# The opening of a two-layer decoder kernel: layer 0's first modulation sums go from VectorE to TensorE, and their tiles' places, the loads and the opening blocks are put in another order

## The chip, the cores and the metric

The kernel runs on one core of one Trainium2 chip. The metric is the device time of one execution in microseconds (us). Engines are named as in the profile: PE (TensorE's products), PEld (its weight loads), DVE (VectorE), ACT (ScalarE), POOL (GpSimd), SP (SyncE, which issues most DMAs).

## The reference, cut to what matters

A decoder trunk of two layers on x of 1024 tokens by 1024 channels, in f32. Every layer begins with an RMS norm, scaled and shifted by numbers that come from a vector c:

```
cond = silu(c)
mod = cond @ ada_w[i] + ada_b[i]              # 1024 -> 3 x 1024
shift, scale, gate = split(mod, 3)
h = rmsnorm(x, norm_g[i]) * (1 + scale) + shift
p = h @ w_in                                  # layer 0: 29 column tiles of 128
...                                           # RWKV-7 heads and chunked gMLP (layer 0), attention (layer 1)
x = x + gate * (y @ w_out)
```

The change concerns the shift and scale of layer 0: a product of the 1024 numbers of cond with a 1024 x 2048 part of ada_w[0]. Nothing of h exists before the first of these sums are there.

## The kernel before, in words

All large products take operands that are split into two float32r parts, hi and lo (hi is the rounded value, lo the rest), and three products (hi x hi, lo x hi, hi x lo) stand for one in f32. Tokens are worked in two halves of 512 (HT). h is kept transposed: 8 row blocks k of 128 channels, each 128 x 512 for a half, in the tiles hi0, lo0, hi1, lo1 of the pool hp (new_hh).

The opening stage stands in the pool st0. The order of PE's instructions is as the code writes it (manual_schedule); on DVE, ACT, POOL and SP a scheduler orders by its own estimate, and the DMAs that are marked keep_in_program_order stay as written. Every engine takes its queue in order.

- xnorm(b) loads 128 tokens of x and scales them by their RMS (squares on ACT, a power on POOL, the scaling at L338 on ACT for b of 4 and above, at L340 on DVE below). xblock(b) transposes blocks 0 to 3 on PE (xtp) and copies them to xT on ACT (L352).
- wpiece(i, g) loads half of one of the four first weight tiles (wr) and splits it: hi on ACT (L358), lo on POOL (L359).
- ada_first(q), q of 0 to 3, makes the sums for two row blocks k = 2q and 2q + 1: four loads of 128 x 1024 (adaraw, four buffers, so that a load waits until DVE has read an earlier one), eight steps on DVE acc = raw * cond + acc (L373 the first, L371 the other seven), and four products adac of acc with a column of ones, which add up the 128 partitions. Three small DVE instructions (L382 to L384) make the columns bcol and scol.
- hbuild(k) makes h of the first half: a scale and shift on DVE (hf, L393), hi on ACT (L388), lo on POOL or DVE (L389).
- first(k) is the opening group: for each of four accumulators (p0, p1, pM, py) three products with row block k, 12 products of 512 columns. It runs for k = 0 to 7.
- hlate(k) makes h of the second half from x blocks 4 to 7: four transposes into one of two PSUM buffers (tag m), hf on ACT (L402) or DVE (L404), then hi and lo as in hbuild.

Behind first(7) the four accumulators are read: lora_evac and krv_evac (shifted, ACT L302, DVE L303; tanh of lora at L315). Then front(0) begins: two products lw and la of lora with wupt, each into a buffer of tag m, th and tha on ACT (L509, L513) that empty them, and a transpose kt. Only behind kt stands the first product of the second half (pproj, gproj), with which the long stream of products starts that lasts to the end of the kernel.

Of the kernel before, what the change touches and what calls it, by code (L numbers as in the profile page):

```python
# [93 lines left out]
def tile_kernel(ctx, tc, x, cons, par, rows, ada, ada0, ew, wup, sgw, sgb, ewo, ow, owo, out, dbg=None):  # L94
# [43 lines left out]
    def pm(name):  # L138
        return ps.tile([P, HT], F32, name=name, tag="m", bufs=2)
# [143 lines left out]
    def new_h():  # L283
        return [new_hh(half) for half in range(2)]

    h = new_h()
# [42 lines left out]
    ws = [[wp.tile([P, KC, P], F32R, name="w" + n, tag="w" + n, bufs=2) for n in ("hi", "lo")] for i in range(2)]  # L329
    ws += [[u1.tile([P, KC, P], F32R, name="w", tag=t, bufs=1) for t in ts] for ts in (("SV", "AR"), ("PA", "BR"))]  # L330
    with tc.tile_pool(name="st0", bufs=1, side="right", reuse_waits="tile") as sp, tc.manual_schedule(engines={nc.tensor.engine}):
        def xnorm(b):
            xt = sp.tile([P, D], F32, name="x0", tag="x", bufs=4)
            d = nc.sync.dma_start(out=xt, in_=x[b * P:(b + 1) * P, :])
            tc.keep_in_program_order(d)
            rs = rms_scale((xt[:, 0:HT], xt[:, HT:D]), sp, pg)
            if b >= 4:
                S.activation(xt, xt, AF.Copy, scale=rs)  # L338
            else:
                V.tensor_scalar(out=xt, in0=xt, scalar1=rs, scalar2=None, op0=ALU.mult)  # L340
            return xt

        xT = sp.tile([P, KC, HT], F32, name="xT")
# [1 line left out]
        def xblock(b):  # L345
            xt = xnorm(b)
            for g in range(2):
                pt = pm("xtp")
                for i in range(4):
                    k = g * 4 + i  # L350
                    transpose(pt[:, i * P:(i + 1) * P], xt[:, k * P:(k + 1) * P], ident)
                S.activation(xT[:, g * 4:g * 4 + 4, b * P:b * P + P], pt.rearrange("p (k t) -> p k t", t=P), AF.Copy)  # L352

        def wpiece(i, g):
            gs = slice(g * 4, g * 4 + 4)
            raw = rt.tile([P, 4, P], F32, name="wr", tag="krv", bufs=6)
            tc.keep_in_program_order(nc.sync.dma_start(out=raw, in_=ew[FIRST[i][0]][:, gs, :]))
            S.activation(ws[i][0][:, gs, :], raw, AF.Copy)  # L358
            G.tensor_tensor(out=ws[i][1][:, gs, :], in0=raw, in1=ws[i][0][:, gs, :].bitcast(F32), op=ALU.subtract)  # L359

        def ada_first(q):
            acc = sp.tile([P, 4, P], F32, name="acc", tag="acc", bufs=2)
            for g in range(4):
                raw = sp.tile([P, 2, 4, P], F32, name="adaraw", tag="adaraw", bufs=4)
                d = nc.sync.dma_start(out=raw, in_=ada0[q][:, g])
                tc.keep_in_program_order(d)
                start_dma[0] = d.ins
                for i in range(2):
                    c = cond[:, 2 * g + i:2 * g + i + 1]
                    if g + i:  # L370
                        V.scalar_tensor_tensor(out=acc, in0=raw[:, i], scalar=c, in1=acc, op0=ALU.mult, op1=ALU.add)  # L371
                    else:
                        V.tensor_scalar(out=acc, in0=raw[:, i], scalar1=c, scalar2=None, op0=ALU.mult)  # L373
            pt = psc("adac")
            for i in range(4):
                mm(pt[:, i:i + 1], lhsT=acc[:, i, :], rhs=ones[:, 0:1], start=True, stop=True)
            ks2 = slice(2 * q, 2 * q + 2)

            def col(name):
                return prm[:, COLS[name] + 2 * q:COLS[name] + 2 * q + 2]  # L380

            V.tensor_tensor(out=bcol[:, ks2], in0=pt[:, 0:2], in1=col("sh0"), op=ALU.add)  # L382
            V.tensor_tensor(out=scol[:, ks2], in0=pt[:, 2:4], in1=col("sc0"), op=ALU.add)
            V.scalar_tensor_tensor(out=scol[:, ks2], in0=scol[:, ks2], scalar=1.0, in1=col("ng0"), op0=ALU.add, op1=ALU.mult)  # L384
# [21 lines left out]

        pts = [pproj("p0"), pproj("p1"), pM(), ps.tile([P, HT], F32, name="py", tag="y", bufs=1)]

        def first(k):
            for i in range(4):  # L410
                whi, wlo = ws[i]
                mm(pts[i], lhsT=whi[:, k, :], rhs=h[0][0][:, k, :], start=(k == 0), stop=False)
                mm(pts[i], lhsT=whi[:, k, :], rhs=h[0][1][:, k, :], start=False, stop=False)
# [2 lines left out]
        for b in range(4):  # L416
            xblock(b)
        xs = []
        ada_first(0)
        hbuild(0, G)  # L420
        hbuild(1, G)
        for i in range(4):
            wpiece(i, 0)
        first(0)
        ada_first(1)
        hbuild(2, G)
        hbuild(3, G)
        for i in range(4):
            wpiece(i, 1)
        xs.append(xnorm(4))  # L430
        xs.append(xnorm(5))
        first(1)
        first(2)
        ada_first(2)
        hbuild(4, G)
        hbuild(5, G)
        xs.append(xnorm(6))
        xs.append(xnorm(7))
        first(3)
# [12 lines left out]
        first(7)  # L452
        hlate(6, True, G)
        hlate(7, False, V)
        for i in range(4):
# [956 lines left out]
```

## Time and profile before

| what | value |
|---|---|
| runs, median (lowest to highest of 3) | 1116.17 us (1114.96 to 1116.32) |
| the profiled execution's own time | 1111.06 us |
| its span | 1109.2 us |
| PE busy, of the span | 1028.4 us, 93% |
| DVE / ACT / POOL busy | 720.3 / 526.6 / 388.7 us |
| mean granted clock of PE | 0.988 |

A row of a timeline gives start, length, engine, line, operation, output<-inputs, shapes and count; in brackets stands how long the engine was idle before it, and what ended that. A row of the waits gives who waited for whom, the sum in us, how often, and the longest. Rows of equal instructions that follow each other are merged, so that the length of a merged row reaches from the first start to the last end.

### The profile page before, as it was taken

How to read it: one execution, taken by the hardware profiler on the slowest of the kernel's cores; microseconds unless marked ns; L12 is line 12 of the kernel's file. 1: busy time of each engine (PE TensorE's matmuls, PEld its weight loads, DVE VectorE, ACT ScalarE, POOL GpSimd, SP SyncE). 2: the span in 40 equal slices, each digit the busy share in tenths (PEclk: the TensorE clock that was granted, in tenths of full speed). 3: DMA queues.
4: the chain of work that ended last, by engine and by line, in shares of the span. 5: the costliest groups of instructions: out<-in, count | busy, mean ns of one | idle time of the engine just before them, and what ended most of it. 6: DMA issues, size and time to landing. Idle time of an engine off the chain costs nothing. (4 is left out here: it accounts for less than half of the span.)

```text
span 1109.2 us, 20591 instructions
## 1 busy us (share of the span) xinstructions
PE 1028.4 (93%) x7800; PEld 838.4 (76%) x7800; DVE 720.3 (65%) x1682; ACT 526.6 (47%) x1252; POOL 388.7 (35%) x490
## 2 busy tenths in 40 slices
PE   3799898899998998988999899999999999999997
PEld 2577676777776776766878688878888888878886
DVE  5975858585869584694744576764565654488754
ACT  4575434554454535444332322335565644487521
POOL 3642414240335122252333200034554544467201
PEclk9899999999999999999999999999999999999999
DMA  8710212122222121123324543321110111252121
GB/s 311 267 27 20 77 59 67 40 66 61 75 79 66 59 87 49 58 69 107 102 80 141 161 143 124 124 72 40 39 39 20 39 38 39 69 171 74 62 93 57
DMA packets 55130, 93.41 MB, mean 84 GB/s; under 512 B 5748, under 2 KB 15988, under 8 KB 55032
## 3 DMA queue, kind: packets, MB, share of 16 engines
q1 hardware_dynamic: 45032, 77.10, 21.5%
q10 hardware_dynamic: 10000, 15.01, 4.2%
q8 instruction: 61, 1.00, 0.4%
q14 instruction: 37, 0.30, 0.1%
HBM read 79.49 MB, written 12.59 MB: 83 GB/s over the span
## 5 line engine op out<-in xcount | busy, mean ns | idle before, releaser
L118 PE MATMUL pproj<-hi,whi 128*128 128x512 f32 x704 | 284.5, 404 | 0.7 <-ACT vt L1177 0.7
L118 PE MATMUL pproj<-lo,whi 128*128 128x512 f32 x704 | 283.6, 403 | 0.0
L118 PE MATMUL pproj<-hi,wlo 128*128 128x512 f32 x704 | 283.5, 403 | 0.0
L246 POOL TENSOR_TENSOR wlo<-wraw,whi 128x512 fp32r<-128x512 f32 x86 | 115.1, 1358 | 181.1 <-ACT whi L245 180.2
L118 PEld LDWEIGHTS pproj<-hi,whi 128*128 128x128 f32 x704 | 133.5, 190 | 26.6 <-issue 1.7
L118 PEld LDWEIGHTS pproj<-hi,wlo 128*128 128x128 f32 x704 | 133.3, 189 | 25.1 <-issue 1.0
L118 PEld LDWEIGHTS pproj<-lo,whi 128*128 128x128 f32 x704 | 133.3, 189 | 24.3 <-issue 0.9
L245 ACT ACTIVATE whi<-wraw 128x512 fp32r<-128x512 f32 x102 | 58.6, 622 | 65.7 <-PE htp L122 31.3
L118 PE MATMUL op<-wo,whi 128*128 128x512 f32 x256 | 80.8, 397 | 0.0
L1213 ACT ACTIVATE Sx<-Sx,nm 128x257 f32<-128x257 f32 (+1 forms) x128 | 62.3, 489 | 27.2 <-DVE nm L1209 25.5
L1209 DVE CUSTOM_DVE_ANT_0 Sx<-pS,bias,nsink 128x256 f32<-128x256 f32 (+1 forms) x128 | 53.4, 463 | 30.1 <-PE pS L118 28.6
L1217 POOL TENSOR_SCALAR Sx<-Sx,rc 128x256 f32<-128x256 f32 (+1 forms) x128 | 60.0, 485 | 25.7 <-DVE rc L1215 23.2
L1229 DVE TENSOR_TENSOR PL<-pT,PH 128x512 fp32r<-128x512 f32 (+1 forms) x64 | 41.6, 654 | 30.0 <-ACT PH L1228 29.5
L118 PEld LDWEIGHTS op<-wo,whi 128*128 128x128 f32 x256 | 48.4, 190 | 11.2 <-issue 0.3
L857 DVE SCALAR_TENSOR_TENSOR adacc<-araw,cond,adacc 128x512 f32<-128x512 f32 x56 | 47.0, 839 | 12.6 <-DMA araw<-ada 12.5
L118 PE MATMUL op<-hi,yl 128*128 128x512 f32 (+1 forms) x136 | 51.8, 381 | 0.4 <-DVE yl L1328 0.4
L118 PE MATMUL op<-hi,yh 128*128 128x512 f32 (+1 forms) x136 | 51.8, 381 | 0.4 <-ACT yh L1327 0.4
L118 PE MATMUL op<-lo,yh 128*128 128x512 f32 (+1 forms) x136 | 51.5, 379 | 0.0
L118 PE MATMUL op<-wo,wlo 128*128 128x512 f32 x128 | 51.2, 400 | 0.0
L213 POOL TENSOR_TENSOR st<-st,nhalf 128x1 f32<-128x1 f32 x16 | 10.4, 650 | 102.6 <-DVE st L212 102.6
L650 DVE TENSOR_TENSOR pr<-Lf,LT 128x2 f32<-128x2 f32 (+14 forms) x120 | 44.2, 368 | 2.6
L1228 ACT ACTIVATE PH<-pT 128x512 fp32r<-128x512 f32 (+1 forms) x64 | 35.7, 563 | 17.5 <-PE pT L1223 16.2
(311 smaller groups left out, 2171.7 us busy)
## 6 DMA issues: line engine op xcount, KB each, us to landing
araw<-ada SPq DMA_DIRECT2D x64, 256.0 KB, 2.8
wraw<-ew SPq DMA_DIRECT2D x50, 256.0 KB, 3.1
wraw<-ow SPq DMA_DIRECT2D x36, 256.0 KB, 3.0
adaraw<-ada SPq DMA_DIRECT2D x16, 512.0 KB, 5.5
x<-x SPq DMA_DIRECT2D x8, 512.0 KB, 7.4
woraw<-ewo SPq DMA_DIRECT2D x16, 256.0 KB, 3.0
xr<-x ACTq DMA_DIRECT2D x16, 256.0 KB, 3.2
wraw<-y0d SPq DMA_DIRECT2D x16, 256.0 KB, 3.2
```

The lines of the kernel that those rows point to most:

```text
L118: last[0] = nc.tensor.matmul(out, lhsT=lhsT, rhs=rhs, **kw).ins
L213: G.tensor_tensor(out=st[:, 3:4], in0=st[:, 2:3], in1=nhalf[:, 0:1], op=ALU.pow)
L245: a = S.activation(hi[:, gs, :], raws[g], AF.Copy)
L246: b = E.tensor_tensor(out=lo[:, gs, :], in0=raws[g], in1=hi[:, gs, :].bitcast(F32), op=ALU.subtract)
L650: V.tensor_tensor(out=pr[:, 0:nc_, 0:i + 1], in0=Lf[:, i:i + 1, 0:i + 1].to_broadcast([P, nc_, i + 1]), in1=LTt[:, 0:nc_, 0:i + 1], op=ALU ...
L857: op = V.scalar_tensor_tensor(out=acc, in0=raw, scalar=cond[:, k:k + 1], in1=acc, op0=ALU.mult, op1=ALU.add)
L1209: V.tensor_tensor_reduce(out=Sx[:, e, off:2 * P], in0=pS3[:, e, 0:nk], in1=bias[e][:, off:], scale=1.0, scalar=nsink[:, hd:hd + 1], op0=AL ...
L1213: S.activation(pr[:, e, off:2 * P + 1], Sx[:, e, off:2 * P + 1], AF.Exp, bias=nm[:, e:e + 1], scale=-1.0, accum_out=sm[:, e:e + 1])
L1217: G.tensor_scalar(out=pr[:, e, off:2 * P], in0=pr[:, e, off:2 * P], scalar1=rc[:, e:e + 1], scalar2=0.5, op0=ALU.mult, op1=ALU.mult)
L1228: S.activation(PH[:, ks, :], pT2[:, ks, :], AF.Copy)
L1229: V.tensor_tensor(out=PL[:, ks, :], in0=pT2[:, ks, :], in1=PH[:, ks, :].bitcast(F32), op=ALU.subtract)
```

## The change

The sums become products. For each of the eight steps a product takes as its stationary operand a 128 x 32 tile of c32, of which the first column is cond's and the others are zero, and as its moving operand the loaded 128 x 512 tile itself. Product j goes to the column group j mod 4, that is to 32 of the 128 partitions of one PSUM tile (adar); two products add up in each group. ACT copies the tile to acc, and the four adac products with the ones add the partitions as before (adac is unchanged). The four loads of one q go to one tile; for q of 1 and 2 that is the place of hi1 and lo1, which hold h of the second half later, so new_hh(1) now stands behind the sixth block.

The loads, the opening blocks and some copies are put in another order or on another engine: the x loads 4 to 7 come behind all of ada0; adac of q = 1, 2, 3 stands in the middle of a block (first(k, mid)); all hlate come behind the seventh block, four before the last block and four after; x blocks 4 to 7 are scaled on DVE; half of the xT copies and half of the wlo pieces go to DVE.

```
-            if b >= 4:
-                S.activation(xt, xt, AF.Copy, scale=rs)
-            else:
-                V.tensor_scalar(out=xt, in0=xt, scalar1=rs, scalar2=None, op0=ALU.mult)
+            V.tensor_scalar(out=xt, in0=xt, scalar1=rs, scalar2=None, op0=ALU.mult)
...
+                if g:
+                    V.tensor_copy(dst, src)
+                else:
+                    S.activation(dst, src, AF.Copy)
...
-            G.tensor_tensor(out=ws[i][1][:, gs, :], in0=raw, in1=ws[i][0][:, gs, :].bitcast(F32), op=ALU.subtract)
+            (V if i % 2 else G).tensor_tensor(out=ws[i][1][:, gs, :], in0=raw, in1=ws[i][0][:, gs, :].bitcast(F32), op=ALU.subtract)
...
-                    if g + i:
-                        V.scalar_tensor_tensor(out=acc, in0=raw[:, i], scalar=c, in1=acc, op0=ALU.mult, op1=ALU.add)
-                    else:
-                        V.tensor_scalar(out=acc, in0=raw[:, i], scalar1=c, scalar2=None, op0=ALU.mult)
+        def ada_load(q):
+            if q in (1, 2):
+                raws = hp.tile([P, 4, 2, 4, P], F32, name="adaraw", tag=("hi1", "lo1")[q - 1])
+            else:
+                raws = sp.tile([P, 4, 2, 4, P], F32, name="adaraw", tag="adaraw", bufs=1)
+            for g in range(4):
+                tc.keep_in_program_order(nc.sync.dma_start(out=raws[:, g], in_=ada0[q][:, g]))
+            adas[q] = raws
+
+        def ada_rows(q):
+            raws = adas[q]
+            pt = pm("adar")
+            for g in range(4):
                 for i in range(2):
+                    j = 2 * g + i
+                    a = j % 4 * 32
+                    mm(pt[a:a + 32, :], lhsT=c32[:, j, :], rhs=raws[:, g, i].rearrange("p a b -> p (a b)"), start=j < 4, stop=j >= 4, tile_position=(0, a))
+            acc = rt.tile([P, 4, P], F32, name="acc", tag="t", bufs=5)
+            S.activation(acc, pt.rearrange("p (a b) -> p a b", a=4), AF.Copy)
+            adas[q] = acc
+
+        def ada_done(q):
+            acc = adas.pop(q)
             pt = psc("adac")
...
-        def first(k):
+        def first(k, mid=None):
             for i in range(4):
+                if i == 2 and mid is not None:
+                    ada_done(mid)
...
-        ada_first(0)
-        hbuild(0, G)
-        hbuild(1, G)
+        ada_load(0)
+        ada_rows(0)
+        ada_done(0)
         for i in range(4):
             wpiece(i, 0)
+        ada_load(1)
+        hbuild(0, V)
+        hbuild(1, G)
         first(0)
-        ada_first(1)
-        hbuild(2, G)
+        ada_load(2)
+        ada_rows(1)
+        first(1, 1)
+        hbuild(2, V)
         hbuild(3, G)
         for i in range(4):
             wpiece(i, 1)
-        xs.append(xnorm(4))
-        xs.append(xnorm(5))
-        first(1)
+        ada_load(3)
         first(2)
-        ada_first(2)
-        hbuild(4, G)
+        ada_rows(2)
+        first(3, 2)
+        for b in range(4, 8):
+            xs.append(xnorm(b))
+        hbuild(4, V)
         hbuild(5, G)
-        xs.append(xnorm(6))
-        xs.append(xnorm(7))
-        first(3)
         first(4)
+        ada_rows(3)
+        first(5, 3)
+        hbuild(6, V)
+        hbuild(7, G)
+        h.append(new_hh(1))
+        first(6)
         hlate(0, True, G)
         hlate(1, True, V)
-        ada_first(3)
-        hbuild(6, V)
-        hbuild(7, G)
         hlate(2, False, G)
         hlate(3, True, V)
-        first(5)
+        first(7)
         hlate(4, True, G)
-        hlate(5, False, G)
-        first(6)
-        first(7)
+        hlate(5, False, V)
         hlate(6, True, G)
         hlate(7, False, V)
```

PE's queue at the second block (k = 1), before: the four adac stand ahead of it, and the sums were made on DVE.

```order
L118 MATMUL adac<-ones,acc 128x1 x4
L118 MATMUL p_132<-hi,whi 128x512
L118 MATMUL p_132<-lo,whi 128x512
L118 MATMUL p_132<-hi,wlo 128x512
L118 MATMUL p_133<-hi,whi 128x512
L118 MATMUL p_133<-lo,whi 128x512
L118 MATMUL p_133<-hi,wlo 128x512
L118 MATMUL pM<-hi,w 128x512
```

The same place now; p_133 and p_134 are here what p_132 and p_133 were, the accumulators p0 and p1.

```order
L118 MATMUL adar<-adaraw,c_129 32x512 x8
L118 MATMUL p_133<-hi,whi 128x512
L118 MATMUL p_133<-lo,whi 128x512
L118 MATMUL p_133<-hi,wlo 128x512
L118 MATMUL p_134<-hi,whi 128x512
L118 MATMUL p_134<-lo,whi 128x512
L118 MATMUL p_134<-hi,wlo 128x512
L118 MATMUL adac<-ones,acc 128x1 x4
L118 MATMUL pM<-hi,w 128x512
```

The sums stand ahead of the block, and adac has moved into its middle, with six products ahead of it and six behind. The blocks k = 3 and k = 5 look the same.

ACT's queue from the reading of the first accumulator (lora) on, before; behind these rows come the DMAs of tri and sgwt and then th<-lw, which empties the buffer that kt waits for.

```order
L302 ACTIVATE lora<-p_132,der 128x512
L302 ACTIVATE krv<-p_133,der 128x512
L302 ACTIVATE krv<-pM,der 128x512
L305 ACTIVATE carry<-p_132,prm 128x1
L315 ACTIVATE lora<-lora 64x512
L302 ACTIVATE krv<-py,der 128x512
L505 ACTIVATE kkn<-krv,prm 128x512
L305 ACTIVATE carry<-p_133,prm 128x1
L402 ACTIVATE hf<-xtp,bcol,scol 128x512
L468 DMA rcon<-cons 128x260
L388 ACTIVATE hi<-hf 128x512
L305 ACTIVATE carry<-pM,prm 128x1
```

The same place now, the first twelve rows (L420 is what L402 was, L406 what L388 was, L529 what L505 was).

```order
L302 ACTIVATE lora<-p_133,der 128x512
L420 ACTIVATE hf<-xtp,bcol,scol 128x512
L302 ACTIVATE krv<-p_134,der 128x512
L302 ACTIVATE krv<-pM,der 128x512
L406 ACTIVATE hi<-hf 128x512 x2
L302 ACTIVATE krv<-py,der 128x512
L305 ACTIVATE carry<-p_133,prm 128x1
L315 ACTIVATE lora<-lora 64x512
L529 ACTIVATE kkn<-krv,prm 128x512
L305 ACTIVATE carry<-p_134,prm 128x1
L305 ACTIVATE carry<-pM,prm 128x1
L420 ACTIVATE hf<-xtp,bcol,scol 128x512
```

And the rows that follow, up to the last ahead of th<-lw (which is L533 now).

```order
L305 ACTIVATE carry<-py,prm 128x1
L406 ACTIVATE hi<-hf 128x512 x2
L492 DMA rcon<-cons 128x260
L420 ACTIVATE hf<-xtp,bcol,scol 128x512
L815 DMA tri<-cons 128x128
L822 DMA sgwt<-sgw 128x256
L406 ACTIVATE hi<-hf 128x512
L824 DMA lnb<-rows 128x128
L664 ACTIVATE LT<-rcon 128x128
L406 ACTIVATE hi<-hf 128x512
L827 DMA bst<-sgb 64x128 x2
```

Between lora and th stand three hf and six hi now, where one hf and one hi stood. From the start of the second half's products on, every engine's order is as it was.

More of the change, by code (lines that the diff above doesn't have):

```diff
@@ L284, in new_h @@
         return [new_hh(half) for half in range(2)]
-    h = new_h()
+    h = [new_hh(0)]
     rfs = ExitStack()
@@ L331, in tile_kernel @@
     with tc.tile_pool(name="st0", bufs=1, side="right", reuse_waits="tile") as sp, tc.manual_schedule(engines={nc.tensor.engine}):
+        c32 = sp.tile([P, 8, 32], F32, name="c32")
+        G.memset(c32, 0.0)
+        V.tensor_copy(c32[:, :, 0:1], cond.unsqueeze(2))
         def xnorm(b):
@@ L335, in xnorm @@
             tc.keep_in_program_order(d)
+            start_dma[0] = d.ins
             rs = rms_scale((xt[:, 0:HT], xt[:, HT:D]), sp, pg)
-            if b >= 4:
-                S.activation(xt, xt, AF.Copy, scale=rs)
-            else:
-                V.tensor_scalar(out=xt, in0=xt, scalar1=rs, scalar2=None, op0=ALU.mult)
+            V.tensor_scalar(out=xt, in0=xt, scalar1=rs, scalar2=None, op0=ALU.mult)
             return xt
@@ L351, in xblock @@
                     transpose(pt[:, i * P:(i + 1) * P], xt[:, k * P:(k + 1) * P], ident)
-                S.activation(xT[:, g * 4:g * 4 + 4, b * P:b * P + P], pt.rearrange("p (k t) -> p k t", t=P), AF.Copy)
+                dst, src = xT[:, g * 4:g * 4 + 4, b * P:b * P + P], pt.rearrange("p (k t) -> p k t", t=P)
+                if g:
+                    V.tensor_copy(dst, src)
+                else:
+                    S.activation(dst, src, AF.Copy)
         def wpiece(i, g):
@@ L358, in wpiece @@
             S.activation(ws[i][0][:, gs, :], raw, AF.Copy)
-            G.tensor_tensor(out=ws[i][1][:, gs, :], in0=raw, in1=ws[i][0][:, gs, :].bitcast(F32), op=ALU.subtract)
-        def ada_first(q):
-            acc = sp.tile([P, 4, P], F32, name="acc", tag="acc", bufs=2)
-            for g in range(4):
[L364 to L367, printed above, removed]
-                for i in range(2):
-                    c = cond[:, 2 * g + i:2 * g + i + 1]
-                    if g + i:
-                        V.scalar_tensor_tensor(out=acc, in0=raw[:, i], scalar=c, in1=acc, op0=ALU.mult, op1=ALU.add)
-                    else:
-                        V.tensor_scalar(out=acc, in0=raw[:, i], scalar1=c, scalar2=None, op0=ALU.mult)
+            (V if i % 2 else G).tensor_tensor(out=ws[i][1][:, gs, :], in0=raw, in1=ws[i][0][:, gs, :].bitcast(F32), op=ALU.subtract)
+        adas = {}
+        def ada_load(q):
[3 more added lines that the diff above has]
+                raws = sp.tile([P, 4, 2, 4, P], F32, name="adaraw", tag="adaraw", bufs=1)
+            for g in range(4):
+                tc.keep_in_program_order(nc.sync.dma_start(out=raws[:, g], in_=ada0[q][:, g]))
[4 more added lines that the diff above has]
+            for g in range(4):
+                for i in range(2):
+                    j = 2 * g + i
[6 more added lines that the diff above has]
+            acc = adas.pop(q)
             pt = psc("adac")
```

## The prediction

> **What bounds the kernel now.** I read the windows first, cut at three places of the timeline: the first product of the opening group (28.01), the first product of that group's last row block (66.32) and the first product of the second half (73.61). The columns are length, then busy time of PE, PEld, DVE, ACT, POOL, then the granted clock and the DMA share.
>
> ```profile
> core 0: us, PE busy (x) PEld busy (x) DVE busy (x) ACT busy (x) POOL busy (x), PEclk, DMA share, GB/s
> 0.00:28.01 28.01, 9.74 (x40) 7.82 (x40) 16.68 (x39) 14.11 (x33) 10.39 (x17) 1.00 0.87 310
> 28.01:66.32 38.31, 31.45 (x133) 24.44 (x133) 34.01 (x49) 21.62 (x40) 23.05 (x17) 0.91 0.58 198
> 66.32:73.61 7.29, 6.15 (x30) 4.00 (x28) 4.22 (x6) 7.29 (x16) 4.10 (x5) 1.00 0.17 48
> 73.61:1109.20 1035.59, 981.03 (x7603) 802.10 (x7601) 665.44 (x1589) 483.55 (x1167) 351.14 (x451) 0.99 0.23 74
> ```
>
> From 73.61 on, PE is busy 981.03 of 1035.59 us. The change leaves PE's order there as it was, so I take a shift of 73.61 to be passed on to the end one to one. Everything is decided ahead of 73.61. In the second window DVE is the fullest engine (34.01 of 38.31), and in the third ACT is busy all the time (7.29 of 7.29). Who waits there is in the list of waits up to 74 us, PE's and then the DMA queue's, and what DVE does is in its groups for the same stretch (mean ns behind the busy time):
>
> ```profile
> PE adac L118 <- DVE acc L371: 4.4, 3, 2.8
> PE adac L118 <- DVE st L211: 3.5, 1, 3.5
> PE lw L118 <- ACT krv L302: 1.0, 1, 1.0
> SPq L365 <- DVE acc L371: 19.9, 9, 4.3
> L371 DVE SCALAR_TENSOR_TENSOR acc<-adaraw,cond,acc 128x512 f32<-128x512 f32 x28 | 29.3, 1047 | 0.7
> ```
>
> DVE's 28 accumulations (29.3 us) are what PE waits for, 4.4 + 3.5 = 7.9 us (the small st of L211 stands right behind them), and the queue holds tiles back 19.9 us for them. That is what the change takes away. It could give back those 7.9 us and the slow clock behind them, if nothing else came last.
>
> **The change, term by term.** I follow PE's queue.
>
> *Term 1, up to the first product.*
>
> ```profile
> 17.41 1.94 PE L122 MATMUL xtp<-con,x 128*128 128x128 f32 x8 [1.29 <-DVE x L340]
> 18.53 0.60 ACT L352 ACTIVATE xT<-xtp 128x512 f32<-128x512 f32 x1 [1.78 <-PE xtp L122]
> 22.11 1.84 PE L118 MATMUL adac<-ones,acc 128*128 128x1 f32 x8 [2.76 <-DVE acc L371]
> 35.31 1.02 PE L118 MATMUL adac<-ones,acc 128*128 128x1 f32 x8 [0.65 <-DVE acc L371]
> L118 PE MATMUL adag<-adacc,ones x8: 589/591/592, 430.6 to 624.5; 128*1 128x512 f32 x8
> 430.59 1.02 PE L118 MATMUL adag<-adacc,ones 128*1 128x512 f32 x2
> 152.91 1.15 PE L118 MATMUL pn<-SV,BR 128*64 128x64 f32 x32 [0.62 <-DVE AR L735]
> ```
>
> The new sums (adar, 8 products of 128x32 by 512 in f32) do not occur before. The nearest row is adag, one such product alone: two records, 1.02 us less the 0.59 of the last gives 0.43 from start to start, so 0.86 a product. Eight in a row cost 6.9 us; four side by side, 1.7. That column groups do run side by side shows in pn: 64 of 512 elements would be 0.054 a record, 1.7 us for 32, and they took 1.15 with the last one's drain in it, so two at a time. Nothing shows four; I take 1.7 because pn loses nothing to sharing, and keep 6.9 as the far end. At the start all this doubles, since the clock is half: the same eight adac records take 1.84 there and 1.02 later. So: last transposes end at 17.41 + 1.94 = 19.4; adar 3.4 and a drain of 0.2 make 23.0; ACT's copy 0.6 (as xT), adac 1.8, together 25.5 with the handovers; then the way from adac to the first product, 2.3 (the next fence has it at 2.6 with DVE held up). First product at 27.8, against 28.01. The DVE chain that goes is replaced by a PE-ACT-PE chain as long: gain 0.2.
>
> [...]
>
> *Term 2, up to the last row block.*
>
> ```profile
> 36.37 0.16 DVE L382 TENSOR_TENSOR bcol<-adac,prm 128x2 f32<-128x2 f32 x1
> 37.66 1.00 DVE L393 TENSOR_SCALAR hf<-xT,scol,bcol 128x512 f32<-128x512 f32 x2
> 38.25 0.64 ACT L388 ACTIVATE hi<-hf 128x512 fp32r<-128x512 f32 x1 [2.77 <-DVE hf L393]
> 38.96 1.31 POOL L389 TENSOR_TENSOR lo<-hf,hi 128x512 fp32r<-128x512 f32 x1 [0.71 <-ACT hi L388]
> 40.32 0.50 PE L118 MATMUL p<-lo,whi 128*128 128x512 f32 x1 [0.86 <-POOL lo L389]
> 46.61 1.84 PE L118 MATMUL adac<-ones,acc 128*128 128x1 f32 x8 [3.50 <-DVE st L211]
> 48.88 0.63 PE L118 MATMUL p<-lo,whi 128*128 128x512 f32 x1
> 49.31 0.63 PE L118 MATMUL p<-hi,wlo 128*128 128x512 f32 x1
> 66.32 0.39 PE L118 MATMUL p<-hi,whi 128*128 128x512 f32 x1
> 66.54 0.39 PE L118 MATMUL p<-lo,whi 128*128 128x512 f32 x1
> 69.04 1.03 PE L122 MATMUL xtp<-con,x 128*128 128x128 f32 x8
> ```
>
> A product of 512 starts every 0.23 us, at half clock every 0.43 (48.88 to 49.31, behind a gap of 3.5). PE's own work in the new order, from 27.8: the first block at half clock 12 x 0.43 = 5.2; second sums 2.5 (between 1.7 and 3.4); blocks 1 to 6, 72 x 0.228 = 16.4; third and fourth sums 3.4; three adac 2.7; sixteen transposes, now ahead of the last block, 1.8. Sum 32.0, so 59.8 with no wait at all. Now the waits. From the end of adac (35.31 + 1.02 = 36.33) to hi at 38.89 pass 2.6 us and to lo at 40.27 3.9. The change puts adac in the middle of a block, so six products (1.4 us) cover part; 1.2 to 2.5 us are left, three times. Ahead of hi stand on ACT the second weight pieces in one case and the squares of x in another, and lo is half on DVE now (shorter), so I take 2.0: 6.0 together (3.6 to 7.5). Four hlate in a row have two buffers for their transposes: about 1.0 for ACT's hf (below). Last block at 66.8 against 66.32: plus 0.5, between -5 and +3.
>
> Covered and costed at nothing: the memset and the copy for c32 (start of the kernel, both engines wait for loads); the copies that go from ACT to DVE and the x scalings that do too (DVE has lost 29.3 us); the x loads moved behind all of ada0.
>
> ```profile
> adaraw<-ada SPq DMA_DIRECT2D x16, 512.0 KB, 5.5
> x<-x SPq DMA_DIRECT2D x8, 512.0 KB, 7.4
> wr<-ew SPq DMA_DIRECT2D x8, 256.0 KB, 7.3
> ```
>
> 24 x 512 KB and 8 x 256 KB are 14.7 MB; at the first window's 310 GB/s the last x lands at 47 us, and it is needed by the transposes above, past 58. If the cover went, each late us would count.
>
> *Term 3, the tail.* Before, the last products of group p end at 66.77 + 0.39 = 67.16, and 6.45 us later the second half starts.
>
> ```profile
> 66.77 0.39 PE L118 MATMUL p<-hi,wlo 128*128 128x512 f32 x1
> 66.24 1.15 ACT L388 ACTIVATE hi<-hf 128x512 fp32r<-128x512 f32 x2
> 67.30 0.67 ACT L302 ACTIVATE lora<-p,der 128x512 f32<-128x512 f32 x1
> 71.13 0.77 ACT L402 ACTIVATE hf<-xtp,bcol,scol 128x512 f32<-128x512 f32 x1
> 72.45 0.69 ACT L509 ACTIVATE th<-lw,der 128x512 f32<-128x512 f32 x1
> 71.10 1.09 PE L118 MATMUL lw<-lora,wupt 64*128 64x512 f32 x2 [1.02 <-ACT krv L302]
> 71.96 1.12 PE L118 MATMUL la<-lora,wupt 64*128 64x512 f32 x2
> 73.20 0.66 PE L122 MATMUL kt<-con,kkn 128*128 128x128 f32 x4
> 73.61 0.48 PE L118 MATMUL pproj<-hi,whi 128*128 128x512 f32 x1
> ```
>
> kt needs the buffer that th empties, and th stands 5.15 us behind lora on ACT, which has no idle time there. In the new order ACT has seven more 128x512 instructions between lora and th: five hi and two hf. Before, six of them were through ahead of lora and one hi came after th. They cost 5 x 0.58 + 2 x 0.72 = 4.3, with LT and a carry that also come ahead of th 4.8. Behind waits PE: lw needs the buffer of the seventh hlate, thus its hf, so PE stands for some 6 us where it stood 1.0. The 3.5 us ahead of 46.61 were enough for half clock, so lw and la (2.2 us) take 1.5 more, and the second half's first products lose about 0.5. Tail: 4.8 + 1.5 + 0.5 = plus 6.8, between 4.3 and 8.5.
>
> **Sum.** -0.2 is inside the second term; 0.5 + 6.8 = 7.3 us longer. The profiled execution took 1111.06 (span 1109.2), 5.1 below the runs' median of 1116.17; I add to each: 1118.4 for that one, and 1116.17 + 7.3 = 1123.5 forecast.
>
> **Rivals.**
> *Faster: the front outruns the tail.* If the six trips hide wholly, the last block starts at 59.8, 6.5 earlier; with the tail at its low end, 4.3, the kernel is 2.2 us faster: 1114.0. It decides at 66.32 - 4.3 = 62.0: the last block must start before that. For it: DVE loses its longest job, and loads no longer wait. Against it: every trip still goes PE, ACT, PE, DVE, ACT, and PE's own work alone fills 59.8. Chance 0.08.
> *A free clock from the first product.* adar and adac keep PE at work for 3.4 + 1.8 us ahead of the opening block. If that releases the clock, the block costs 2.7 instead of 5.2: 2.5 less, 1121.0, inside the range, and still slower. Before, the clock was first free behind that block (the same adac at 22.11 and at 35.31), and nothing shows whether adar counts. Chance 0.15, within the forecast's own. [...]
>
> *The column groups do not all run together.* Two at a time, each sum takes 1.7 more, the first 3.4: 3.4 + 3 x 1.7 = 8.5 more, 1132; one at a time, (6.9 - 1.7) x 5 = 26 more, 1149.5. For it: only pairs show in the trace. Against: the pairs are perfect. Chance 0.10, most of it for pairs.
> *Nothing to see.* The front gains what the tail loses: 1116. Chance 0.07.
>
> **How the numbers follow.** Forecast 0.75; by the bounds of terms 2 and 3 it goes from -0.7 to +11.5, and without the low end, where a front without waits would have to meet the shortest tail, from 1118 to 1128. The range reaches on to pairs of column groups, 1132, and down to 1117.5; it leaves out the faster case, nearly all of the same case, and one at a time. Within 0.2% (2.2 us, about what a measurement of this kernel can tell from no change): 0.07. Slower by more: 0.75 + 0.10 = 0.85. Faster by more: 0.08.
>
> **What would show it.** Right: the first product near 28, the last block's first product between 64 and 69, ACT without idle time from lora to th for about 10 us, PE idle ahead of lw for over 4, half clock there, pproj near 81, and from there an unchanged distance to the end. adar should be 16 records in about 1.9 us, 3.6 the first time. Wrong: adar at 3.5 or more at full clock; a last block before 62; lw within 5 us of the end of the last block; or a later part of the kernel whose distance to pproj changes by over 1 us.

## The result, and the profile after

| kernel | median us (lowest to highest, runs) | before, beside it | ratio, 95% interval |
|---|---|---|---|
| changed | 1118.65 (1117.69 to 1121.23, 9) | 1116.12 (1112.20 to 1116.66, 9) | 1.0031 [1.0017, 1.0045] |
| changed, second comparison (e9 below) | 1118.12 (1117.52 to 1119.27, 5) | 1113.54 (1111.55 to 1116.50, 17) | 1.0039 [1.0027, 1.0052] |

The change makes the kernel slower, by 0.3 to 0.4%: 3.5 and 4.3 us at 1115 us. The forecast was slower by 7.3 us (0.65%). The time lies inside the range, near its low end. The two profiled executions stand further apart than the runs: 1118.93 against 1111.06, spans 1117.0 against 1109.2.

The windows of the changed kernel, cut at the same three places (first product of the opening group, of its last row block, of the second half), with the columns of before:

```profile
0.00:26.75 26.75, 11.96 (x56) 7.71 (x56) 12.00 (x35) 12.76 (x30) 6.61 (x16) 0.99 0.95 365
26.75:66.19 39.44, 35.01 (x172) 22.53 (x173) 13.92 (x33) 15.17 (x34) 10.79 (x10) 0.92 0.43 166
66.19:79.72 13.53, 9.60 (x39) 6.07 (x38) 8.95 (x12) 11.91 (x25) 7.02 (x7) 0.78 0.12 34
79.72:1117.00 1037.28, 984.60 (x7602) 804.01 (x7600) 664.49 (x1589) 483.27 (x1163) 350.99 (x450) 0.99 0.23 74
```

DVE has lost its long job (34.01 us in the second window before, 13.92 now), and still the last row block begins at 66.19, as it did at 66.32. The third window, from the last block to the second half, has grown from 7.29 to 13.53 us, at a clock of 0.78. PE's rows show both halves of this:

```profile
19.98 3.23 PE L118 MATMUL adar<-adaraw,c 128*32 128x512 f32 x16
23.94 1.05 PE L118 MATMUL adac<-ones,acc 128*128 128x1 f32 x8 [0.73 <-ACT acc L387]
26.75 0.80 PE L118 MATMUL p<-hi,whi 128*128 128x512 f32 x1 [1.76 <-ACT hi L406]
40.13 0.50 PE L118 MATMUL p<-hi,whi 128*128 128x512 f32 x1 [1.68 <-ACT hi L406]
41.13 0.50 PE L118 MATMUL p<-lo,whi 128*128 128x512 f32 x1 [0.50 <-DVE lo L407]
54.21 1.92 PE L118 MATMUL adar<-adaraw,c 128*32 128x512 f32 x16
66.19 0.48 PE L118 MATMUL p<-hi,whi 128*128 128x512 f32 x1
66.74 0.39 PE L118 MATMUL p<-hi,wlo 128*128 128x512 f32 x1
73.54 1.70 PE L122 MATMUL xtp<-con,x 128*128 128x128 f32 x8 [3.30 <-DVE hf L422]
75.87 2.07 PE L118 MATMUL lw<-lora,wupt 64*128 64x512 f32 x2 [0.63 <-ACT hf L420]
78.96 1.11 PE L122 MATMUL kt<-con,kkn 128*128 128x128 f32 x4
79.72 0.78 PE L118 MATMUL pproj<-hi,whi 128*128 128x512 f32 x1
```

A sum is 16 records in 1.92 us (3.23 the first time, from 19.98 on, where the first record of a full clock stands at 22.67). PE waits a little behind each adac, and then 3.30 us in the tail for an hf; lw behind that takes 2.07 us for 1.09, kt 1.11 for 0.66. ACT, in the same stretch, goes from lora to th in 10.98 us (5.15 before) with pauses of 0.32, 0.17 and 0.59 only at its end:

```profile
67.17 0.69 ACT L302 ACTIVATE lora<-p,der 128x512 f32<-128x512 f32 x1 [0.40 <-PE p L118]
75.04 0.78 ACT L420 ACTIVATE hf<-xtp,bcol,scol 128x512 f32<-128x512 f32 x1 [0.32 <-DVE lo L407]
76.94 0.63 ACT L406 ACTIVATE hi<-hf 128x512 fp32r<-128x512 f32 x1 [0.17 <-DVE hf L422]
78.15 0.69 ACT L533 ACTIVATE th<-lw,der 128x512 f32<-128x512 f32 x1 [0.59 <-PE lw L118]
```

### The profile page after: what moved, and what is told of

Its sections match the earlier page's. It is cut to its first block, busy times and chain, and to the rows that moved or that the text cites. A ratio compares the mean times of both kernels' runs of the same rounds, so it can differ in the third digit from the quotient of the medians.

```text
span 1117.0 us, 20669 instructions
## 1 busy us (share of the span) xinstructions
PE 1041.2 (93%) x7864; PEld 840.3 (75%) x7864; DVE 699.4 (63%) x1667; ACT 523.1 (47%) x1248; POOL 375.4 (34%) x483
## 3 DMA queue, kind: packets, MB, share of 16 engines
q8 instruction: 62, 1.02, 0.4%
HBM read 79.49 MB, written 12.59 MB: 82 GB/s over the span
## 4 chain that ended last, share of the span: by engine, by line
PE 72%; DVE 14%; ACT 6%; issue 2%; POOL 1%; DMA 1%; ACTq 0%; POOLq 0%; SPq 0%; DVEq 0%
PE pproj L118 36%; PE op L118 16%; PE pS L118 2%; PE po L118 2%; PE pT L1247 2%; PE pM L118 2%; DVE pr L674 2%; ACT Dg L656 1%; PE py L118 1%; PE uw L118 1%; DVE LT L675 1%; PE pn L118 1%; PE chain L118 1%; PE A L118 1%; PE p L118 1%
## 5 line engine op out<-in xcount | busy, mean ns | idle before, releaser
L118 PEld LDWEIGHTS op<-wo,whi 128*128 128x128 f32 x256 | 48.6, 190 | 11.3 <-issue 0.3
```

The lines of the kernel that those rows point to most:

```text
L118: last[0] = nc.tensor.matmul(out, lhsT=lhsT, rhs=rhs, **kw).ins
```

## The experiments

All differences in us are the ratio to the kernel before, taken at 1114. "Tail" is the time from the first product of the last row block to the first pproj.

**e1, the kernel before once more.** No edit.

> The kernel before, with nothing changed; it is to show what an ordinary execution of it looks like. The profiled execution that the prediction was worked out from took 1111.06 us, the runs some 1116, and the changed kernel's two agree (1118.93 and 1118.65). Theory: the profiled execution of before was a lucky one, because fewer of the 3.4 us windows of its clock fell to half; an ordinary one has its first product of the second half (pproj) near 73.6 us as well, a mean clock nearer 0.983 than 0.988, and loses the 4 to 5 us in half-clock windows scattered over the kernel: about 1116. Rival: an ordinary execution already loses 3 us or more in the opening, pproj at 76.5 or later, so that the opening of before is dearer than the profile showed and the change's tail is paid against that. Ratio to the kernel before 1.000 within 0.15%.

Measured: median 1114.94, ratio 0.9999 [0.9982, 1.0016]; its runs go from 1111.11 to 1117.73, and the 23 beside it from 1109.85 to 1118.42. Its profiled execution took 1113.32:

```profile
28.25:67.19 38.94, 32.02 (x133) 24.79 (x133) 34.04 (x49) 22.58 (x41) 23.89 (x18) 0.83 0.58 202
67.19:74.48 7.29, 6.15 (x30) 4.00 (x28) 4.27 (x6) 6.41 (x14) 3.25 (x5) 1.00 0.17 48
74.48:1111.50 1037.02, 983.53 (x7603) 803.26 (x7601) 665.08 (x1589) 484.13 (x1167) 352.16 (x451) 0.99 0.24 74
```

The tail is 7.29 to the hundredth. The window ahead of it took 38.94 where it took 38.31, and what follows took 1037.0 for 1035.6. So the theory holds for the most part: 1111.06 was one of the shortest executions that this kernel has, and pproj at 74.48 is far from the rival's 76.5. The clocks of the two profiles can't be compared as they stand. A trace counts a clock of 1.00 until its first record of the granted clock. That record stands at 14.32 in e1 but only at 34.90 in before, where the products up to 34 us are 0.63 long, as at half clock (0.39 or 0.40 from 36.52 to 39.06). With that stretch counted, the window of before has a clock of 0.82, like e1's 0.83 and not 0.91. Without the 17.07 us at half clock that only e1 counts, its mean of 0.976 would be 0.984, near the expected 0.983. The 1116.17 of the first three runs stood above the medians of all four later comparisons (1113.54 to 1115.0).

**e2, the late hlate alone.** The kernel before with

```
         first(4)
-        hlate(0, True, G)
-        hlate(1, True, V)
         ada_first(3)
...
-        hlate(2, False, G)
-        hlate(3, True, V)
         first(5)
-        hlate(4, True, G)
-        hlate(5, False, G)
         first(6)
+        hlate(0, True, G)
+        hlate(1, True, V)
+        hlate(2, False, G)
+        hlate(3, True, V)
         first(7)
+        hlate(4, True, G)
+        hlate(5, False, V)
```

> The kernel before with one part of the change alone: all eight hlate stand behind the seventh block, four ahead of the last block and four behind it; the sums stay on DVE. Theory (the tail's price is what the change costs): the distance from the end of p to pproj grows from 6.45 to about 13 us, ACT is busy from lora to th for about 11 us instead of 5.15, and the last block starts within 1.5 us of 66.3, so the time is 5 to 8 us over before's. Rival (late hlate cost nothing by themselves, it is the sums' round trips that cost): distance under 9 us, time within 2 us of before's. A third reading (lost in the front, because blocks no longer fill DVE's waits): the last block is more than 2 us later and the distance stays near 6.5.

Measured: 1125.95, ratio 1.0099 [1.0074, 1.0124], 11.0 us over before.

```profile
68.69 0.48 PE L118 MATMUL p<-hi,whi 128*128 128x512 f32 x1
78.33 2.07 PE L118 MATMUL lw<-lora,wupt 64*128 64x512 f32 x2 [1.21 <-ACT hf L402]
83.02 0.78 PE L118 MATMUL pproj<-hi,whi 128*128 128x512 f32 x1
```

The tail is 14.33, 7.0 longer than before's, and ACT goes from lora to th in 11.10 us, as the theory has it. Beyond the theory, the last block comes 1.5 to 2.4 us later too: the hlate had filled the waits for DVE's sums (PE waits 10.9 us ahead of adac, 7.9 in before). The remaining 2 us lie in the second half, which took longer here (1044.3 us from pproj on) than in any other profile, but the profiled execution, at 1129.06, is also the longest of the six.

**e3, the sums alone.** The changed kernel with the blocks and the hlate in the order of before (ada_load, ada_rows and ada_done stand where ada_first stood).

> The changed kernel with the blocks, the x loads and the hlate in the order of before: only the sums are products (with the smaller moves of copies between ACT and DVE). Theory: the tail is before's, so the distance from the end of p to pproj is 6 to 7 us; the front gains little, since each sum still goes PE, ACT, PE, DVE, ACT, DVE or POOL before the next block: last block at 64.5 to 67, time between 3 us under and 1 us over before's. Rival (the DVE sums were what held PE, 7.9 us of waits): last block before 61, time 5 us or more under before's. Rival (the sums as products cost more than they save): last block after 68, time 2 us or more over before's.

Measured: 1111.05, ratio 0.9966 [0.9952, 0.9980], 3.8 us under before, a little more than the theory's 3. Its PE rows:

```profile
66.02 0.39 PE L118 MATMUL p<-hi,whi 128*128 128x512 f32 x1
70.85 1.09 PE L118 MATMUL lw<-lora,wupt 64*128 64x512 f32 x2 [1.07 <-DVE hf L422]
```

The first pproj stands at 73.31, a tail of 7.29 again. The sums gain, the late hlate lose: the change holds both. But the opening shows only a small part of the gain. It is 0.3 us shorter than in before's profile and 1.2 shorter than in e1's; where the rest of the 3.8 us comes from is not shown.

**e4, the sums without column groups.**

```
-        c32 = sp.tile([P, 8, 32], F32, name="c32")
+        c32 = sp.tile([P, 8, P], F32, name="c32")
...
-                    a = j % 4 * 32
-                    mm(pt[a:a + 32, :], lhsT=c32[:, j, :], ..., start=j < 4, stop=j >= 4, tile_position=(0, a))
+                    mm(pt, lhsT=c32[:, j, :], ..., start=j == 0, stop=j == 7)
```

> The changed kernel with stationary tiles of 128 columns (the first is cond's, the others zero) instead of 32: the eight products of one sum accumulate one behind the other in one PSUM tile, no column groups. Theory (four groups run fully side by side, a sum costs 1.7 us at full clock against 6.9 in a row): adar takes about 6.9 us a sum at full clock and 10 or more the first time, 5 us more for each of the three later sums and up to 7 for the first; the three waits behind adac (1.7, 1.1, 0.5 us in the changed kernel) cannot cover that, so the time is 15 to 22 us over the changed kernel's. Rival (the groups are not what makes the sum short; the moving tile's read is the limit): adar within 1 us of the changed kernel's, time unchanged. Rival (PE kept busy by the longer sums runs at full clock earlier): only 8 to 14 us more.

Measured: 1134.40, ratio 1.0188 [1.0165, 1.0212]: 20.9 us over before, some 17 over the changed kernel, as the theory has it.

```profile
19.69 8.21 PE L118 MATMUL adar<-adaraw,c 128*128 128x512 f32 x16
36.34 7.03 PE L118 MATMUL adar<-adaraw,c 128*128 128x512 f32 x16
```

7.03 against 1.92: four groups side by side are 3.7 times as fast, and this is the price of their not being so. The first sum, expected at 10 us or more, took 8.21: the trace grants full clock from 21.91 on, within it.

**e5 and e6, the two openings alone.** Behind the evacuation of the four accumulators stand only the copy kkn, lw, th, la, tha, kt, 24 products of the second half, and the writes.

> Only the opening of the kernel before: it ends with the first 24 products of the second half (pproj) and writes their tile sixteen times; all that follows is left out, so its time stands beside that of the opening of the changed kernel, not beside a whole kernel's. The profiled executions put pproj at 73.61 and 79.72 us, 6.1 apart; the whole kernels' runs are only some 3.5 apart. Theory (the whole kernel before, profiled at 1111.06 and 1113.32, mostly runs at 1114 to 1116, because its PE waits for DVE let the clock fall for a varying number of 3.4 us windows in the opening): this opening's runs are spread over 3 us or more, and its median stands only 2 to 4.5 us below the changed opening's. Rival (the opening takes what the profiles show, and what differs lies later in the kernel): spread under 2 us, and 5.5 to 7 us below the changed one's.

> Only the opening of the changed kernel, cut in the same place; what follows is left out. Theory (sums as products leave PE no long wait ahead of the tail, so the clock stays up from 33 to 74 us): runs within 2.5 us of each other. Median against that of the opening of before: 2 to 4.5 us more by the theory, 5.5 to 7 more by the rival.

Measured: 95.17 (94.96 to 96.37, 4 runs) and 101.90 (101.34 to 102.17, 4 runs): 6.7 us apart, pproj at 73.10 and 79.52. The rival has it: the opening costs what the profiles show. The spread of 1.4 us in the opening of before is not the 8 us of the whole kernel.

**e7, the tail's pauses filled.**

```
         hlate(5, False, V)
+        fill(3)
         hlate(6, True, G)
         hlate(7, False, V)
+        fill(2)
```

> The changed kernel with five f32 products of ident and wupt (0.86 us each at full clock, into the PSUM tile of the squares, which nobody reads) in the pauses of PE's tail: three ahead of the seventh hlate, where PE waits 3.3 us, and two behind the eighth. They do nothing but keep PE at work. Theory (the pause costs twice: ACT's and DVE's queue, and half clock behind it for lw, la, kt and the first pproj, 2 us): lw at full clock, from p's end to pproj 10.3 to 11.3 us instead of 12.7, time 1.5 to 2.5 us under the changed kernel's, still over before's. Rival (the half clock is hidden, since th waits for ACT anyway): pproj and time within 0.7 us of the changed kernel's.

Measured: 1114.09, ratio 1.0015 [1.0000, 1.0031], 1.7 us over before, 1.8 to 2.6 under the changed kernel.

```profile
64.52 0.48 PE L118 MATMUL p<-hi,whi 128*128 128x512 f32 x1
68.40 2.74 PE L118 MATMUL fill<-wupt,con 128*128 128x512 f32 x6
74.61 1.12 PE L118 MATMUL lw<-lora,wupt 64*128 64x512 f32 x2
77.25 0.47 PE L118 MATMUL pproj<-hi,whi 128*128 128x512 f32 x1
```

lw takes 1.12 for 2.07, so the half clock behind the pause was real (0.50 from 73.87 to 80.69 in the changed kernel): from lw to pproj pass 2.64 us, 3.85 in the changed kernel. The last two fillers push lw back by 0.4, so the tail shrinks by 0.8 only (12.73 for 13.53), and from p's end to pproj pass 11.8 us, more than the 10.3 to 11.3 of the theory. The rest of the gain lies behind pproj (1033.2 us to the end for 1037.3).

**e8, the sums earlier, the hlate near their old places.** An excerpt of the edit:

```
                 if i == 2 and mid is not None:
-                    ada_done(mid)
+                if i == 1 and mid is not None:
+                    ada_rows(mid)
+                if i == 3 and mid is not None:
+                    ada_done(mid)
...
+        first(0, 1)
...
+        first(2, 2)
...
+        first(4, 3)
...
         hlate(0, True, G)
         hlate(1, True, V)
+        first(5)
         hlate(2, False, G)
         hlate(3, True, V)
+        first(6)
+        hlate(4, True, G)
+        hlate(5, False, G)
         first(7)
...
```

> A kernel put together from what the parts showed: the sums are products as in the changed kernel, but each stands one block earlier (eight products ahead of the second accumulator of blocks 0, 2 and 4, adac ahead of the fourth), so that the copy to acc and the way from adac to h run beside products; all hlate stand where they stand in the kernel before. Theory (the sums' gain is the front's, the loss is the late hlate's, and the two are independent): no wait ahead of adac, last block at 60 to 64 us, p's end to pproj 6 to 7.5 us, time 4 to 9 us under before's and under that of the sums alone (0.34% under before). Rival (the round trips only move to another wait, or loads come too late for the earlier sum): last block after 65, time no better than the sums alone.

The text above has all hlate where they stand in the kernel before. In this kernel hlate(2) to hlate(5) stand one block later, the first two of them behind the sixth block and the other two behind the seventh.

Measured: 1109.11, ratio 0.9956 [0.9939, 0.9973], 4.9 us under before: better than before and than the changed kernel. That it also beats the sums alone (e3, 0.9966 [0.9952, 0.9980]) is not shown, since the intervals overlap.

```profile
59.89 0.48 PE L118 MATMUL p<-hi,whi 128*128 128x512 f32 x1
65.41 0.66 PE L118 MATMUL lw<-lora,wupt 64*128 64x512 f32 x1 [1.66 <-DVE hf L422]
68.49 1.12 PE L122 MATMUL kt<-con,kkn 128*128 128x128 f32 x4 [1.74 <-ACT th L533]
69.26 0.78 PE L118 MATMUL pproj<-hi,whi 128*128 128x512 f32 x1
```

Ahead of the three later adac no wait stands in its trace (ahead of the first, 0.73 us), and the last block begins 6.4 us earlier than before's. Of that the tail takes 2.1 back (9.37), more than was expected: PE reaches lw and kt before the hf and th they wait for. How much of that is owed to the four hlate that stand a block later was not tested.

**e9 to e11, a second comparison, and a pure delay.** e9 is the changed kernel; e10 and e11 are the kernel before with five or eight idle products ahead of lw:

```
             FIRST[i][1](0, pts[i])
+        pf = pg("fill")
+        for i in range(8):
+            mm(pf, lhsT=ident, rhs=wupt, start=True, stop=True)
```

> The changed kernel with nothing changed, beside the two kernels below. The openings alone, cut at the same place, take 95.17 and 101.9 us: the change costs 6.7 us there. Reading A (a shift of the opening is passed on one to one, and the first comparison was a loose one, since the runs of the kernel before spread over 8 us): 5 to 7 us over before, ratio 1.0045 to 1.0063. Reading B (what follows the opening gives 2 to 4 us of it back, every time): ratio 1.002 to 1.004 again. In its profile the first product of the second half stands at 79.0 to 80.5.

> The kernel before with a pure delay: five f32 products of ident and wupt, 0.86 us each, ahead of lw on PE, so that the second half starts 3.3 us later (4.3 less the 1.0 for which PE waits there anyway), with PE at full clock and every other engine free. Nothing else moves. Reading A (passed on one to one): 2.8 to 3.8 us over before. Reading B (the other engines, which go on during the pause, stand further ahead and later waits shrink): under 2 us. Reading C (what follows takes a time of its own that hangs on where the 3.4 us windows of the clock fall on its pauses, so that a shift changes it by steps of about 1.6 us in either direction): off 3.3 by 1.5 or more.

> The same with eight products: the second half starts 5.9 us later, close to what the change does to it. Reading A: 5.4 to 6.4 us over before, and twice what three us of delay cost. Reading B: under 4 us. Reading C: off 5.9 by 1.5 or more, not in proportion to the shorter delay.

Measured: e9 1.0039 (table above); e10 1114.87, ratio 1.0007 [0.9995, 1.0018], 0.8 us; e11 1119.68, ratio 1.0050 [1.0037, 1.0064], 5.6 us. With e9, reading B holds once more (pproj at 79.20 in its profile), though the interval reaches to reading A's 1.0045. The tails of e10 and e11 are 10.29 and 12.87, so PE was in fact held up by 3.0 and 5.6 us. The longer delay comes through whole, of the shorter one 2 us are missing; reading B, which fits the shorter delay, fails on the longer. Where such pieces go, the same two stretches of the second half (cut within 0.6 us of the 801st, 1001st and 1201st pproj) show, in before, e9, e10 and e11:

```profile
414.52:509.50 94.98, 83.97 (x900) 64.13 (x898) 64.00 (x129) 46.41 (x103) 34.09 (x26) 0.98 0.20 65
509.50:592.31 82.81, 78.39 (x795) 62.29 (x794) 45.47 (x110) 28.86 (x67) 25.14 (x21) 0.98 0.33 103
```

```profile
419.78:517.37 97.59, 86.56 (x900) 66.46 (x898) 64.34 (x130) 46.19 (x102) 34.56 (x26) 0.95 0.21 63
517.37:597.71 80.34, 76.98 (x800) 61.27 (x796) 45.25 (x110) 29.11 (x67) 25.18 (x22) 1.00 0.34 106
```

```profile
417.02:515.02 98.00, 88.00 (x900) 66.79 (x898) 64.30 (x130) 46.35 (x102) 34.48 (x26) 0.93 0.20 63
515.02:595.43 80.41, 77.00 (x800) 61.28 (x796) 45.24 (x110) 29.11 (x67) 25.17 (x22) 1.00 0.34 106
```

```profile
420.80:515.81 95.01, 83.90 (x899) 64.14 (x898) 64.03 (x129) 46.23 (x102) 34.32 (x26) 0.98 0.21 65
515.81:596.02 80.21, 76.83 (x795) 61.18 (x794) 45.38 (x110) 28.94 (x67) 25.16 (x21) 1.00 0.34 106
```

The same instructions take 95.0 us at a granted clock of 0.98 and 97.6 or 98.0 at 0.95 or 0.93; the next stretch takes 80.3 or 82.8. A stretch loses 2 to 3 us or does not, and where it does its granted clock is the lower one. That fits reading C (its steps of about 1.6 us were the author's estimate; a window of 3.41 us at a clock of 0.50, as in the rows further down, would cost 1.7), though e11, whose delay comes through whole, shows that the sum of such pieces need not be off.

**e12 and e13, what makes the tail long.** Four buffers for hf instead of two, and the hf of the sixth hlate on ACT:

```
-            hf = lp.tile([P, HT], F32, name="hf", tag="tp", bufs=2)
+            hf = (lp if k % 2 else sp).tile([P, HT], F32, name="hf", tag="tp" if k % 2 else "hf", bufs=2)
```

```
-        hlate(5, False, V)
+        hlate(5, True, V)
```

> The changed kernel with four instead of two buffers for hf of the hlate (even k take the two that hbuild no longer needs). Nothing else is touched: ACT has the same instructions. Theory of the prediction (the tail is as long as ACT's queue between lora and th, which is full): lw and pproj move by less than 0.7 us (in the changed kernel's profiles 75.3 to 75.9 and 79.2 to 79.7), time within 1 us of the changed kernel's (0.35% over before). Rival (an hf has to wait until lo of the one two before it is through, so that each pair makes a round trip ACT, DVE or POOL, ACT, and ACT's queue only looks full because everything in it waits its turn): lw 1.5 to 2.5 us earlier, pproj at 76.5 to 78, time 1.5 to 4 us under the changed kernel's.

> The changed kernel with the hf of the sixth hlate on ACT instead of DVE: one 128x512 instruction more for ACT between lora and th, one less for DVE. Theory of the prediction (ACT's count sets the tail): pproj 0.7 to 1 us later. Rival (DVE holds PE, since the longest wait there, 3.30 us, is for this hf on DVE, behind the four steps of the evacuation): pproj 1 us or more earlier. Third reading (the round trip through two buffers sets it, and on ACT this hf stands behind more copies): pproj 1.5 to 2.5 us later.

Measured: e12 1112.91, ratio 0.9995 [0.9981, 1.0009], some 4 us under the changed kernel; e13 1117.61, ratio 1.0034 [1.0020, 1.0047]. The tails are 11.13 and 15.09, where the changed kernel has 13.53 (13.52 in e9). Rows of e12, ACT's first, and of e13:

```profile
64.74 0.77 ACT L420 ACTIVATE hf<-xtp,bcol,scol 128x512 f32<-128x512 f32 x1
65.40 0.63 ACT L406 ACTIVATE hi<-hf 128x512 fp32r<-128x512 f32 x1
65.92 0.69 ACT L302 ACTIVATE lora<-p,der 128x512 f32<-128x512 f32 x1
73.89 0.69 ACT L533 ACTIVATE th<-lw,der 128x512 f32<-128x512 f32 x1
```

```profile
64.27 0.48 PE L118 MATMUL p<-hi,whi 128*128 128x512 f32 x1
69.42 1.46 PE L122 MATMUL xtp<-con,x 128*128 128x128 f32 x8 [1.26 <-DVE hf L422]
75.40 0.78 PE L118 MATMUL pproj<-hi,whi 128*128 128x512 f32 x1
```

```profile
65.66 0.48 PE L118 MATMUL p<-hi,whi 128*128 128x512 f32 x1
77.13 1.22 PE L118 MATMUL lw<-lora,wupt 64*128 64x512 f32 x1 [2.31 <-ACT hf L420]
80.75 0.78 PE L118 MATMUL pproj<-hi,whi 128*128 128x512 f32 x1
```

With four buffers the tail is 2.4 us shorter, and ACT goes from lora to th in 7.97 us instead of 10.98. ACT has the same instructions as in the changed kernel, but not in the same order: one hf and one hi that stood behind lora now run ahead of it (the first two rows), and LT comes behind th, at 78.38. By their spacing (0.66, 0.52 and some 0.3 us) these three make up half of the 3.0 us. Of the rest, 1.08 us are ACT's three pauses, of which none is left. So the two buffers did lengthen the tail, by the pauses and by the order that came with them. ACT is still full between lora and th, and PE still waits 1.26 and 0.91 us for DVE's hf. Moving one hf to ACT costs 1.6 in the tail, twice its own 0.78, as the third reading has it: one of ACT's pauses, for DVE's lo, grows to 1.46 us. Both speak for the round trip through the buffers beside ACT's work; DVE's queue as the only cause falls, since the tail grew when DVE was relieved. (The time of e13 does not show its 1.6: 3.8 us over before, like the changed kernel.) Where the changed kernel's front starts a little earlier or later, the place of pproj moves with it (e12's group starts at 25.17), which is why the tails are compared and not the places.

## Why the direction was right, and which step of the prediction was wrong

- **Direction and mechanism: right.** The hlate moved behind the sixth and seventh block are what costs (e2: 11.0 us alone, e8 and e3: a gain as soon as they stand among the blocks again). ACT has hardly a pause for 11 us, PE stands idle for 3.9 us behind the last block (3.30 and 0.63, "over 4" was forecast), lw and la run at half clock (2.07 us for lw, 1.09 before), pproj comes at 79.7 ("near 81").
- **Term 1's gain was too small (0.2; it was 1.3).** The first product came at 26.75, and at 26.37 and 26.54 in e9 and e6, not at 27.8: behind adar the clock is full, so adac takes 1.05 and not 1.84. The rival of a free clock is half right: the clock was full from 22.67 to 26.08, but the opening block itself still runs at half clock (0.50) until 32.91, with products of 0.63 us. In the traces of before and of the changed kernel the changes of the granted clock stand 3.41 us or a multiple of it apart, and these are the windows between them (the 1.00 of the first row only says that no record stands there yet; adar's 3.23 us in it show half clock):

```profile
19.30:22.71 3.41, 3.41 (x20) 0.95 (x18) 2.50 (x3) 2.61 (x5) 2.28 (x2) 1.00 1.03 417
22.71:26.12 3.41, 1.56 (x16) 0.97 (x8) 2.25 (x6) 0.65 (x2) 0.68 (x1) 0.99 1.02 406
26.12:29.53 3.41, 2.78 (x6) 1.95 (x7) 1.07 (x2) 1.10 (x2) 1.27 (x1) 0.50 1.04 394
29.53:32.94 3.41, 3.41 (x12) 2.01 (x14) 0.00 (x0) 0.00 (x0) 0.00 (x0) 0.50 1.04 411
```

 Behind the window full of PE's work the clock was full (0.99); behind the one with 1.56 us of work it was half (0.50), behind the one with 2.78 still half, and behind the next full one full again (1.00 from 32.91 on). In e1 the clock was still full behind a window with 1.77 us of work (41.62 to 45.04): adac at 46.84 takes 1.02. By what the clock is granted, these rows do not show.
- **Term 2 came out right (66.19 for 66.8) by errors that cancel, which is luck.** Its start was 1.0 us early. The waits behind adac are 2.18 (the rows at 40.13 and 41.13), 1.32 and 0.50, and 0.43 for the hlate: 4.4 us, not 7.0. PE's own work is 39.44 - 4.43 = 35.0 us, not 32.0: the first block takes 5.7 instead of 5.2, blocks with adac in the middle take 3.9 instead of 3.6, and blocks behind a wait 3.1 to 3.2 instead of 2.7.
- **The price of a sum was right:** 1.9 at full clock for 1.7 and a drain. Four groups are 3.7 times as fast as products one behind the other (7.03 us in e4, 1.92 here).
- **Term 3 was near in size (6.1 for 6.8), wrong in part of its reason.** From p's end (66.74 + 0.39 = 67.13) to pproj pass 12.59 us, 6.1 more than before. ACT from lora to th takes 5.8 more: 4.75 of work, as was counted (4.8), and 1.08 of pauses, which were not. The half clock is there (e7), but shows as some 1 us, not 2.0: 0.59 is ACT's last pause, for lw, and from th to pproj pass 0.4 us more than before. And the two buffers, booked with 1.0 among the first hlate, lengthen the tail itself by 2.4, in part through ACT's order (e12).
- **The step that failed is the way from the opening to the time:** that a shift of pproj is "passed on to the end one to one". The opening is 6.1 us longer in the profiled pair and 6.7 in e5 and e6, not far from the 7.3 of the sum, and the time grew by only 3.5 to 4.3. Other kernels do not pass their shift on either: e10's 3.0 us of pure delay became 0.8, and e3's opening is 0.3 to 1.2 shorter, its time 3.8; e11's 5.6 came through whole. From pproj to the end of the span the profiled executions took 1035.6 (before), 1037.0 (e1), 1037.3 (changed), 1036.7 (e9), 1038.2 (e10), 1035.2 (e11), 1033.2 (e7) and 1034.6 (e12); e3, e4, e8 and e13 lie between, at 1036.0 to 1037.5, and with e2 it was 1044.3. So that stretch is not a constant but has 2 or 3 us of its own either way. It goes broadly with the time at half clock that the traces record there: 14.3 us in e7, 19.6 in before, 26.9 in the changed kernel, 36.0 in e10 (37.3 in e2, too little more to explain its 1044.3). The prediction named a change of over 1 us there as a sign of being wrong, and the profiled pair shows 1.7. That this pair stands 7.9 us apart, near the 7.3, is luck: 6.1 of the opening and 1.7 of that stretch. Against e1 the changed kernel's e9 has pproj 4.7 us later and a span 4.4 us longer.
- **What stays open:** why the two whole kernels differ by 2 to 3 us less than their openings cut out, and why e3 gains 3 us more than its opening. The order of instructions behind pproj is not the reason in e3, where that of PE, DVE, ACT and POOL is before's. In the changed kernel PE's is too, and on the other three a few instructions right behind pproj change places. The differences in the granted clock are large enough (the same instructions took 95.0 us at 0.98 and 98.0 at 0.93), and a pure delay of 3.0 us also lost 2 of them; but that the openings of the kernels send what follows into a different clock each time was argued, not shown run by run.

## What to carry to other kernels

Work that is moved off a full engine gains only what its round trip leaves, and the work that used to fill that engine's waits has to stay in them: the kernels with the sums as products and hlate among the blocks (e3, e8) were 0.3 to 0.4% faster, though e3's opening shows only a small part of that, and the change lost about twice as much by heaping the transposes of the next stage at the end, behind two buffers. In a queue without pauses, ask which instructions a buffer keeps there and which belong there. A forecast to 0.3% should not rest on a single profiled execution: look at the spread of the runs first, and give a long stretch that is "unchanged" its own width in the range.

## What the hardware showed that was not expected

- Four column groups of 32, each 512 columns in f32, run side by side almost without loss: 16 records in 1.92 us, against 7.03 one behind the other.
- The clock was full for a single window of 3.41 us (22.67 to 26.08) and then half again, as in the rows above. About the same wait ahead of adac left adac at half clock in before (3.50 us idle, adac 1.84) and at full clock in e1 (3.45 us idle, adac 1.02). In before the clock fell at 45.14, ahead of that adac; in e1 the first products of 0.63 us stand behind it, from 48.54 on.
- The clock behind the first transposes was not the same in two executions of one kernel. In e1 PE ran nothing up to 14.32 but the first sixteen f32 transposes (4.01 us), and the four from 14.33 on took 0.63 us. In before the same sixteen took 4.02 us, and the next eight 1.94, as at half clock (eight take 1.03 at 69.04). PE is busy for 8.93 of the first 28.25 us in e1, and for 9.74 of the first 28.01 in before.
- One program has levels: nine of e7's twelve runs took 1112.4 to 1115.1 us at mean clocks of 0.986 to 0.989, three took 1118.3 to 1119.2 at 0.981. The changes of the clock stand at different places in the two profiles of the changed kernel (22.67, 26.08 and 32.91; 22.05, 25.46 and 32.28 in e9). What e7's levels come from is not shown.
